# b cast to bf16 before its transposes, transposed as 4-byte words of two k each, with four rows of b in each partition

## The chip, the cores and the metric

The kernel runs on one core of one Trainium2 chip. A time is the device time of one execution in microseconds (us), the median of several runs; a span is that of the profiled execution, from its first to its last instruction, and is 1.6 to 2 us shorter. The kernel before takes 129.39 us (129.38 to 129.58, 3 runs). Engines are named as the profile names them: PE (TensorE matmuls), PEld (its weight loads), DVE (VectorE), ACT (ScalarE), POOL (GpSimd), SP (SyncE, which only issues DMAs here). On one core a run is told to be slow when it is over 1.5% above the fastest of its kernel.

## The reference

```python
batch, m, k, n = 16, 512, 512, 512
a: (batch, k, m) float32        b: (batch, n, k) float32
out = np.matmul(a.transpose(0, 2, 1), b.transpose(0, 2, 1)).astype(np.float32)
```

So out[m, n] is the sum over k of a[k, m] b[n, k]. The kernel's matmuls contract over partitions, so its tiles of both have k there. a has k first and is loaded as it is; b has n first, and the kernel transposes it on the chip. Per batch 1 MiB of a and 1 MiB of b come in, and 1 MiB goes out.

## The kernel before

Four k lie in each partition of a (`k = 4 ki + ko`). Rows of b lie 128 apart in a partition (`n = 128 no + ni`), so that a partition reads four separate runs of 2 KB. PE transposes b in f32, 16 times 128x128 per batch. DVE takes the transposes out of PSUM and casts them to bf16. ACT casts a. ACT and DVE take turns with the output.

```python
b_v = b.rearrange("b (no ni) k -> b ni no k", ni=P)
# a_pool 3, b_pool 3, ac_pool 4, bt_pool 3, o_pool 8, psum_t 4, psum_o 4 buffers; LAG = 6
for i in range(B):
    # ... b_sb and a_sb are loaded by DMA from SP; ACT casts a_sb to a_bf, four times 128x512
    b_sr = b_sb.rearrange("p no (pk rk) -> p no rk pk", rk=KO)
    for rk in range(KO):
        bt_ps = psum_t.tile([P, N], f32)
        for no in range(NO):
            nc.tensor.transpose(bt_ps[:, no * P:(no + 1) * P], b_sr[:, no, rk, :], identity)
        nc.vector.tensor_copy(bt_sb[:, rk, :], bt_ps)           # DVE, L73
    for rm in range(MO):
        for rk in range(KO):
            nc.tensor.matmul(o_ps, a_br[:, rk, rm, :], bt_sb[:, rk, :], ...)   # PE, L80
        # rm even: ACT copies o_ps to o_sb; rm odd: DVE does (L90)
    if i >= LAG:
        emit_out_dma(i - LAG)
```

Of the kernel before, what the change touches and what calls it, by code (L numbers as in the profile page):

```python
# [1 line left out]

# [5 lines left out]


@with_exitstack
def kernel(
    ctx: ExitStack,
    tc: tile.TileContext,
    a: bass.AP,
    b: bass.AP,
    out: bass.AP,
):
    nc = tc.nc
    P = 128  # L20
    B, K, M = a.shape
    _, N, _ = b.shape
    KO = K // P
    MO = M // P
    NO = N // P

    f32 = mybir.dt.float32
    cdt = mybir.dt.bfloat16

    a_v = a.rearrange("b (ki ko) m -> b ki ko m", ko=KO)  # L30
    b_v = b.rearrange("b (no ni) k -> b ni no k", ni=P)
    out_v = out.rearrange("b (mi mo) n -> b mi mo n", mo=MO)

    const = ctx.enter_context(tc.tile_pool(name="const", bufs=1))
    identity = const.tile([P, P], f32)
    make_identity(nc, identity)

    a_pool = ctx.enter_context(tc.tile_pool(name="a_pool", bufs=3))
    b_pool = ctx.enter_context(tc.tile_pool(name="b_pool", bufs=3))
    ac_pool = ctx.enter_context(tc.tile_pool(name="ac_pool", bufs=4))  # L40
    bt_pool = ctx.enter_context(tc.tile_pool(name="bt_pool", bufs=3))
    o_pool = ctx.enter_context(tc.tile_pool(name="o_pool", bufs=8))
    psum_t = ctx.enter_context(tc.tile_pool(name="psum_t", bufs=4, space=bass.MemoryType.PSUM))
    psum_o = ctx.enter_context(tc.tile_pool(name="psum_o", bufs=4, space=bass.MemoryType.PSUM))

    LAG = 6
    o_tiles = {}

    def emit_out_dma(j):
        nc.sync.dma_start(out_v[j], o_tiles.pop(j))  # L50

    for i in range(B):
        b_sb = b_pool.tile([P, NO, K], f32)
        nc.sync.dma_start(b_sb, b_v[i])
        a_sb = a_pool.tile([P, KO, M], f32)
        nc.sync.dma_start(a_sb, a_v[i])  # L56

        a_bf = ac_pool.tile([P, KO, M], cdt)
        for rk in range(KO):
            nc.scalar.copy(a_bf[:, rk, :], a_sb[:, rk, :])  # L60
        a_br = a_bf.rearrange("p rk (pm rm) -> p rk rm pm", rm=MO)

        b_sr = b_sb.rearrange("p no (pk rk) -> p no rk pk", rk=KO)
        bt_sb = bt_pool.tile([P, KO, N], cdt)
        for rk in range(KO):
            bt_ps = psum_t.tile([P, N], f32)
            for no in range(NO):
                nc.tensor.transpose(  # L68
                    bt_ps[:, no * P:(no + 1) * P],
                    b_sr[:, no, rk, :],  # L70
                    identity,
                )
            nc.vector.tensor_copy(bt_sb[:, rk, :], bt_ps)  # L73

        o_sb = o_pool.tile([P, MO, N], f32)
        o_tiles[i] = o_sb
        for rm in range(MO):
            o_ps = psum_o.tile([P, N], f32)
            for rk in range(KO):
                nc.tensor.matmul(  # L80
                    o_ps,
                    a_br[:, rk, rm, :],
                    bt_sb[:, rk, :],
                    start=(rk == 0),
                    stop=(rk == KO - 1),
                )
            if rm % 2 == 0:
                nc.scalar.copy(o_sb[:, rm, :], o_ps)  # L88
            else:
                nc.vector.tensor_copy(o_sb[:, rm, :], o_ps)  # L90

        if i >= LAG:
            emit_out_dma(i - LAG)

    for j in range(B - LAG, B):
        emit_out_dma(j)


# [1 line left out]
_INS = ['a', 'b']  # L100
_OUTS = [((16, 512, 512), 'float32')]


# [23 lines left out]
```

## Time and profile before

| | before |
|---|---|
| time, median | 129.39 us |
| span | 127.8 us |
| DMA: bytes, mean rate | 50.42 MB, 394 GB/s |
| busy share PE, DVE, ACT | 72%, 48%, 43% |
| packets of 2 KB | 8192, median 84 ns each |
| packets of 8 KB | 4105, median 309 ns each |

The packet figures are from the DMA packet records of the trace. The page's busy lines (tenths in 40 slices of the span) and its queue line show a DMA queue that is hardly ever idle:

```profile
PE   0099999999999995768767796877779777670000
DMA  3999999999999999999999999999999999999980
q1 hardware_dynamic: 13056, 50.33, 97.5%
```

The costliest groups of the same page, with busy us and mean ns of one:

```profile
L80 PE MATMUL o_ps<-bt_sb,a_bf 128*128 128x512 bf16 x248 | 59.0, 385 | 9.1 <-ACT a_bf L60 8.7
L73 DVE CAST bt_sb<-bt_ps 128x512 bf16<-128x512 f32 x64 | 40.0, 683 | 14.7 <-PE bt_ps L68 14.7
L68 PE MATMUL bt_ps<-identity,b_sb 128*128 128x128 f32 x256 | 35.7, 295 | 12.8 <-DMA b_sb<-in_b_dram 12.8
```

The list of waits (us in total, times, longest) says who sets the pace: ACT waits for a, and the transposes wait for b, that is for DMA.

```profile
ACT a_bf L60 <- DMA a_sb<-in_a_dram: 39.5, 13, 6.8
PE bt_ps L68 <- DMA b_sb<-in_b_dram: 12.8, 9, 6.4
```

In the first third data is there early, and the chain of waits (start us, us, what) shows what a batch takes when PE alone limits: 1.92 us of transposes and 3.45 us of matmuls, with nothing between them.

```profile
35.80 1.92 PE bt_ps L68 x16
37.72 0.22 PE o_ps L80
37.94 0.05 issue
37.99 3.18 PE o_ps L80 x14
41.18 1.92 PE bt_ps L68 x16
```

That is 5.4 us against some 7.5 us per batch of DMA.

### The profile page before, as it was taken

The page shows a single profiled execution, that of the slowest core. Times are in us where ns is not written, and L with a number is a line of the kernel's source. Part 1 is how long each engine was busy: PE and PEld are TensorE (multiplying, and loading weights), DVE is VectorE, ACT ScalarE, POOL GpSimd, SP SyncE. Part 2 cuts the span into 40 slices and gives each one's busy share as a digit, 9 for nine tenths or more (in the row PEclk, how much of TensorE's full clock was granted, in tenths as well). Part 3 has the DMA queues.
Part 4 walks back from the last instruction along what each step waited for, and adds up shares of the span by engine and source line. Part 5 has one row for each costly group of instructions (what it writes and reads, how often), then busy time and mean ns, then how long its engine had stood idle before and what let it go on. Part 6 is the DMA issues. An engine that isn't in the chain of part 4 may idle for free.

```text
span 127.8 us, 1405 instructions
## 1 busy us (share of the span) xinstructions
PE 92.5 (72%) x504; PEld 60.6 (47%) x512; DVE 61.5 (48%) x96; ACT 54.8 (43%) x97; POOL 0.7 (1%) x6
## 2 busy tenths in 40 slices
PE   0099999999999995768767796877779777670000
PEld 0094858678586763364634536353364634430000
DVE  0053668586774865463544727355472635640000
ACT  4026747646674635407163460816337072540000
POOL 2000000000000000000000000000000000000000
PEclk9999999999999999999999999999999999998555
DMA  3999999999999999999999999999999999999980
GB/s 90 402 370 422 406 399 420 382 409 398 404 417 415 417 419 394 416 410 429 420 410 423 406 436 405 416 426 413 427 402 431 412 424 418 426 428 428 426 346 36
DMA packets 13063, 50.42 MB, mean 394 GB/s; under 512 B 768, under 2 KB 768, under 8 KB 8960
## 3 DMA queue, kind: packets, MB, share of 16 engines
q1 hardware_dynamic: 13056, 50.33, 97.5%
q8 instruction: 4, 0.07, 0.2%
q14 instruction: 3, 0.02, 0.0%
HBM read 33.55 MB, written 16.78 MB: 394 GB/s over the span
## 4 chain that ended last, share of the span: by engine, by line
DMA 50%; PE 34%; SPq 3%; ACT 1%; issue 1%; DVE 1%; ACTq 0%
DMA a_sb<-in_a_dram 32%; PE o_ps L80 22%; DMA out_dram<-o_sb 13%; PE bt_ps L68 12%; DMA b_sb<-in_b_dram 4%; SPq L56 3%; ACT a_bf L60 1%; DVE o_sb L90 1%; ACT o_sb L88 0%; ACTq L60 0%; SPq L50 0%
## 5 line engine op out<-in xcount | busy, mean ns | idle before, releaser
L80 PE MATMUL o_ps<-bt_sb,a_bf 128*128 128x512 bf16 x248 | 59.0, 385 | 9.1 <-ACT a_bf L60 8.7
L60 ACT CAST a_bf<-a_sb 128x512 bf16<-128x512 f32 x64 | 34.9, 615 | 39.6 <-DMA a_sb<-in_a_dram 39.5
L73 DVE CAST bt_sb<-bt_ps 128x512 bf16<-128x512 f32 x64 | 40.0, 683 | 14.7 <-PE bt_ps L68 14.7
L68 PE MATMUL bt_ps<-identity,b_sb 128*128 128x128 f32 x256 | 35.7, 295 | 12.8 <-DMA b_sb<-in_b_dram 12.8
L80 PEld LDWEIGHTS <-a_bf 128*128 128x128 bf16 x256 | 27.3, 115 | 35.8 <-ACT a_bf L60 17.7
L68 PEld LDWEIGHTS bt_ps<-identity,b_sb 128*128 128x128 f32 x256 | 33.9, 211 | 17.5 <-PE o_ps L80 8.5
L90 DVE COPY o_sb<-o_ps 128x512 f32<-128x512 f32 x32 | 22.1, 692 | 38.9 <-PE o_ps L80 21.9
L88 ACT COPY o_sb<-o_ps 128x512 f32<-128x512 f32 x32 | 18.8, 586 | 19.0 <-PE o_ps L80 18.9
L60 ACT ACT_TABLE_LOAD x1 | 1.3, 1283 | 0.7 <-PEq L111 0.7
masks.py:199 POOL TENSOR_SCALAR_AFFINE_SELECT identity<-identity 128x128 f32<-128x128 f32 x1 | 0.3, 292 | 0.1
masks.py:197 POOL MEMSET identity<- 128x128 f32 x1 | 0.2, 204 | 0.3 <-POOLq L111 0.3
L111 POOL MEMSET const-bfloat16-1.0<- 128x1 bf16 x1 | 0.1, 101 | 0.0
L111 POOL MEMSET const-uint8-127<- 128x1 uint8 x1 | 0.1, 101 | 0.0
L111 POOL MEMSET const-float32-0.0<- 128x1 f32 x1 | 0.1, 98 | 0.2 <-issue 0.2
L111 POOL MEMSET const-float32-1.0<- 128x1 f32 x1 | 0.1, 98 | 0.0
## 6 DMA issues: line engine op xcount, KB each, us to landing
b_sb<-in_b_dram SPq DMA_DIRECT2D x16, 1024.0 KB, 15.4
a_sb<-in_a_dram SPq DMA_DIRECT2D x16, 1024.0 KB, 17.3
out_dram<-o_sb SPq DMA_DIRECT2D x16, 1024.0 KB, 17.4
```

The source lines that it names most:

```text
L56: nc.sync.dma_start(a_sb, a_v[i])
L60: nc.scalar.copy(a_bf[:, rk, :], a_sb[:, rk, :])
L68: nc.tensor.transpose(bt_ps[:, no * P:(no + 1) * P], b_sr[:, no, rk, :], identity,)
L73: nc.vector.tensor_copy(bt_sb[:, rk, :], bt_ps)
L80: nc.tensor.matmul(o_ps, a_br[:, rk, rm, :], bt_sb[:, rk, :], start=(rk == 0), stop=(rk == KO - 1),)
L88: nc.scalar.copy(o_sb[:, rm, :], o_ps)
L90: nc.vector.tensor_copy(o_sb[:, rm, :], o_ps)
L111: nc = _bacc.Bacc("TRN2", target_bir_lowering=False, num_devices=1)
```

## The change

The intent is to halve the transposes. DVE first casts b to bf16. Two neighbouring bf16 values are then read as one 4-byte word, and a transpose of such words moves two k at once: 8 transposes per batch and 2 evictions, not 16 and 4. The matmuls read each half of the words at a 4-byte step. Besides, b's rows now lie four to a partition (`n = 4 ni + no`), so that a partition reads one run of 8 KB. That leaves the transposed columns in another order, and the eviction puts them right by writing at a 16-byte step. Buffer counts and the lag of the stores change too.

```diff
-    b_v = b.rearrange("b (no ni) k -> b ni no k", ni=P)
+    b_v = b.rearrange("b (ni no) k -> b ni no k", no=NO)
-    # a_pool 3, b_pool 3, ac_pool 4, o_pool 8, LAG 6          (cut: five lines)
+    # a_pool 5, b_pool 5, ac_pool 3, bc_pool 2, o_pool 6, LAG 3
-        b_sr = b_sb.rearrange("p no (pk rk) -> p no rk pk", rk=KO)
-        bt_sb = bt_pool.tile([P, KO, N], cdt)
-        for rk in range(KO):
-            bt_ps = psum_t.tile([P, N], f32)
+        bc = bc_pool.tile([P, NO, K], cdt)
+        nc.vector.tensor_copy(bc, b_sb)
+        bc_w = bc.bitcast(f32).rearrange("p no (pk j) -> p no j pk", j=KO // 2)
+        bt_sb = bt_pool.tile([P, KO // 2, N], f32)
+        bt_w = bt_sb.rearrange("p j (ni no) -> p j no ni", no=NO)
+        for j in range(KO // 2):
+            bt_ps = psum_t.tile([P, NO, P], f32)
             for no in range(NO):
-                nc.tensor.transpose(bt_ps[:, no * P:(no + 1) * P], b_sr[:, no, rk, :], identity)
-            nc.vector.tensor_copy(bt_sb[:, rk, :], bt_ps)
+                nc.tensor.transpose(bt_ps[:, no, :], bc_w[:, no, j, :], identity)
+            nc.vector.tensor_copy(bt_w[:, j, :, :], bt_ps)
+        bt_h = bt_sb.bitcast(cdt).rearrange("p j (n h) -> p j h n", h=2)
...
-                    bt_sb[:, rk, :],
+                    bt_h[:, rk // 2, rk % 2, :],
```

## The prediction

> **What bounds the kernel now.** DMA. The page's DMA line is at 9 tenths in every slice but the first and last, the one data queue took 97.5% of the time of its 16 engines, and 50.33 MB moved at 394 GB/s over the 127.8 us span. PE (72%), DVE (48%) and ACT (43%) have slack: from 60 us on the timeline's period is 7.5 us per batch, set by "ACT a_bf waits for DMA a_sb" (39.5 us in all, the largest wait), in which PE works about 5.9 us. The chain passes through PE for 34%, but before 44 us, where DMA is full too.

> **On the bound.** No byte less moves. But b's rows are taken four to a partition, which reads one run of 8 KB, not four of 2 KB: 8192 packets of 2 KB become 2048 of 8 KB, like those of a and of the output. The trace's packet records have medians of 84 ns for 2 KB (mean 86.2) and 309 ns for 8 KB (mean 312.7). These fit 9 ns fixed + 37.5 ns per KB, and a 4-byte semaphore packet indeed takes 9 ns. [...] Saving per MiB of b: 4 x 84 - 309 = 27 ns per 8 KB by medians (32 by means), x 2048 / 16 engines = 3.5 to 4.1 us. All of that is on the limit.

> **Off the bound.** Transposes: 256 become 128, 120 ns each when dense (1.92 us for 16 in the chain): about 1 us of PE per batch saved. PSUM evictions by DVE: 64 become 32, now f32 written at a 16-byte step (0.68 us each if the step costs nothing). Added: a DVE cast 128x2048 f32 to bf16 in SBUF[...], per batch. DVE stays near 4 to 5 us per batch, under the 7.3 us of DMA. The output matmuls now read their moving operand at a 4-byte step; I expect 215 ns each as now. None of this is on the bound, so halving the transposes earns almost nothing.

> Buffers: only 8 DMAs are in flight (each issue waits for the landing of the eighth before it), so five input buffers can't be used fully. With LAG 3, stores 12 to 14 (about 7.4 us) cover the last batch's compute, which took 5.2 us from landing to store issue; so no bubble.

> **Predicted time.** 129.4 - 3.5 to 4.1 = 125.3 to 125.9 (pure stores ran at 428 GB/s, so a little more is possible). I say 125.2 us, 80% range 122.8 to 127.4. Chances: faster by over 2% 0.80, within 2% 0.12, slower 0.08.

> **What would show it right.** 6144 data packets of 8 KB at about 309 ns; none of 2 KB; mean GB/s 405 to 412; DMA still at 9 tenths throughout; PE's share near 60%; the wait "ACT a_bf for DMA a_sb" larger still; [...] L85 matmuls with unchanged mean.

> **What would make it wrong.** (1) The 4-byte step halves the matmul's rate: 16 x 0.43 + 1 = 8 us per batch, above DMA's 7.3; then PE bounds it, about 137 us. (2) Stores interleaved earlier with loads slow both, as in slices around 40 us, where 8 KB packets took 318 ns. (3) The last store waits for compute and leaves DMA idle. (4) More packets overlap, and it falls to 123.

The 9 ns are the trace's own. So are the 8 DMAs in flight: in the trace of before every issue came after the landing of the eighth before it, by 0.06 us at the closest (51.51 us, after 51.45). DVE's "4 to 5 us per batch" is a sum with the cast's term in it: the terms left, two evictions of transposes at 0.68 us and two output evictions at 0.69 us (the trace of before), make 2.7 us.

## More of the kernel before

The program text doesn't fix in which order an engine gets its instructions. The framework's scheduler settles that when the kernel is built, and the listing of the built kernel shows the outcome.

PE goes from one batch into the next by itself: while DVE still empties PSUM, the next transposes read b straight from the tile that DMA filled.

## The result

The changed kernel takes 141.05 us (median of 4 runs, 141.03 to 142.13) against 129.40 us for the kernel before in the same rounds: ratio 1.0925, interval 1.0888 to 1.0962. It is slower by some 9%; its output is correct. A ratio here and below is the recorded one of the two kernels' fast runs in the same rounds, and not quite the ratio of the medians quoted.

The page of after. Compare the DMA line: it is full as before for 32 slices, and then falls into holes. The second line is the TensorE clock that the throttle granted, in tenths.

```profile
PE   0099797884793947749385583957749395674940
PEclk9999999999689996899959999599999959999599
DMA  4999999999999999999999999999999980707016
q1 hardware_dynamic: 6912, 50.33, 87.0%
```

The packet records have 6154 packets of 8 KB with a median of 309 ns (and three longer records), and none of 2 KB. By the ends of these packets 90% of the bytes had moved at 110.4 us, against 112.8 us before: up to there DMA is ahead of the kernel before. The last 10% take 29 us. What is late is output.

```profile
L85 PE MATMUL o_ps<-bt_sb,a_bf 128*128 128x512 bf16 x249 | 70.8, 437 | 11.6 <-DVE bt_sb L77 10.3
L76 PE MATMUL bt_ps<-identity,bc 128*128 128x128 f32 x128 | 19.8, 300 | 31.6 <-DVE bc L67 31.6
L77 DVE COPY bt_sb<-bt_ps 128x512 f32<-128x512 f32 x32 | 31.7, 1066 | 12.6 <-PE bt_ps L76 12.6
L67 DVE CAST bc<-b_sb 128x2048 bf16<-128x2048 f32 x16 | 19.5, 1218 | 5.9 <-DMA b_sb<-in_b_dram 5.9
```

The transposes take half of what they took, 19.8 us and not 35.7 us. But each batch's first one now waits for the cast on DVE (31.6 us in all), and ACT and DVE hardly wait for DMA any more:

```profile
PE bt_ps L76 <- DVE bc L67: 31.6, 15, 6.9
ACT a_bf L60 <- DMA a_sb<-in_a_dram: 6.3, 2, 6.0
DVE bc L67 <- DMA b_sb<-in_b_dram: 5.9, 2, 5.5
```

The chain of waits between 58.98 and 75.93 us (two batches, from one cast to the next) shows a closed ring:

```profile
58.98 1.23 DVE bc L67
60.20 0.14 issue
60.34 0.73 PE bt_ps L76 x4
61.07 0.02 issue
61.09 1.08 DVE bt_sb L77
62.17 0.04 issue
62.21 3.81 PE o_ps L85 x16
66.02 0.02 issue
66.05 0.03 DVE o_sb L95
66.08 0.57 issue
66.66 1.23 DVE bc L67
...
69.89 3.34 PE o_ps L85 x8
73.23 0.23 issue
73.45 1.84 PE o_ps L85 x7
75.29 0.02 issue
75.32 0.04 DVE o_sb L95
75.35 0.57 issue
75.93 1.23 DVE bc L67
```

The cast of batch i+1 (1.23) is followed by its first four transposes (0.73), their eviction (1.08), the 16 matmuls (3.81) and DVE's last output eviction of that batch (0.69; the chain books 0.57 of it as "issue", and the next cast starts 0.08 before its recorded end). Only then comes the next cast. The listing of the built kernel shows why, and the trace has the same order: from batch 4 on, DVE's order is cast, two evictions of transposes, two output evictions, cast. The next b has landed long before (the cast waits for DMA only twice, at the start), but it stands in the queue behind an eviction that waits for PE, and PE's next transposes wait for the cast. In this trace each such cast starts within 0.1 us of the eviction's end, though its b had landed (as an example, batch 8's b at 59.97 us; its cast started at 66.66 us).

One turn of the ring takes 7.68 us, and 9.27 us where the clock was at half for 3.4 us, so that the matmuls took 5.4 us and not 3.8 (69.89 to 75.29). DMA's period would be some 7.4 us (an estimate: 3 MiB at the 425 GB/s of the middle slices).

### The profile page after: what moved, and what is told of

Same layout as the page of the kernel before. It is cut to its first block, busy times and chain, and to the rows that moved or that the text cites. A ratio compares the mean times of both kernels' runs of the same rounds, so it can differ in the third digit from the quotient of the medians.

```text
span 139.1 us, 1115 instructions
## 1 busy us (share of the span) xinstructions
PE 90.4 (65%) x377; PEld 46.7 (34%) x384; DVE 71.9 (52%) x80; ACT 53.4 (38%) x97; POOL 0.7 (1%) x6
## 3 DMA queue, kind: packets, MB, share of 16 engines
q1 hardware_dynamic: 6912, 50.33, 87.0%
## 4 chain that ended last, share of the span: by engine, by line
PE 55%; DVE 26%; issue 9%; DMA 5%; ACT 1%; SPq 0%
PE o_ps L85 48%; DVE bc L67 12%; DVE bt_sb L77 12%; PE bt_ps L76 7%; DMA a_sb<-in_a_dram 5%; DVE o_sb L95 1%; ACT a_bf L60 1%; SPq L54 0%
## 5 line engine op out<-in xcount | busy, mean ns | idle before, releaser
L85 PE MATMUL o_ps<-bt_sb,a_bf 128*128 128x512 bf16 x249 | 70.8, 437 | 11.6 <-DVE bt_sb L77 10.3
L85 PEld LDWEIGHTS <-a_bf 128*128 128x128 bf16 x256 | 30.9, 121 | 48.1 <-issue 27.5
L76 PE MATMUL bt_ps<-identity,bc 128*128 128x128 f32 x128 | 19.8, 300 | 31.6 <-DVE bc L67 31.6
L77 DVE COPY bt_sb<-bt_ps 128x512 f32<-128x512 f32 x32 | 31.7, 1066 | 12.6 <-PE bt_ps L76 12.6
L76 PEld LDWEIGHTS bt_ps<-identity,bc 128*128 128x128 f32 x128 | 17.2, 209 | 38.3 <-issue 36.6
L67 DVE CAST bc<-b_sb 128x2048 bf16<-128x2048 f32 x16 | 19.5, 1218 | 5.9 <-DMA b_sb<-in_b_dram 5.9
```

The source lines that it names most:

```text
L67: nc.vector.tensor_copy(bc, b_sb)
L76: nc.tensor.transpose(bt_ps[:, no, :], bc_w[:, no, j, :], identity)
L77: nc.vector.tensor_copy(bt_w[:, j, :, :], bt_ps)
L85: nc.tensor.matmul(o_ps, a_br[:, rk, rm, :], bt_h[:, rk // 2, rk % 2, :], start=(rk == 0), stop=(rk == KO - 1),)
```

## The experiments

Theory A: the loss is that ring; the place of the cast in DVE's order closes it, the lowered clock makes it longer. Rival B: the stepped reads and writes, with a clock that falls of itself. Rival C: the buffer counts and the earlier stores. Besides: is the DMA gain real? All kernels gave correct results.

| label | time, us | ratio to before |
|---|---|---|
| e1_cast_ahead | 126.75 | 0.980 |
| e2_warm | 135.93 | 1.050 |
| e3_old_pools | 134.11 | 1.034 |
| e4_rows_only | 134.22 | 1.038 |
| e5_two_casts | 165.13 | 1.277 |
| e6_words_only | 132.54 | 1.023 |
| e7_ahead_lag6 | 126.04 | 0.975 |
| e8_step_only | 129.59 | 1.002 |
| e9_rows_out_read | 126.43 | 0.978 |
| e10_rows_psum_step | 126.55 | 0.978 |
| e11_bc3 | 140.08 | 1.087 |
| e12_cast_pool | 127.11 | 0.982 |

The kernel before measured 129.24 to 129.57 us beside them. Each kernel ran 4 times (e7_ahead_lag6 5 times); one run of e3_old_pools and the profiled one of e12_cast_pool were slow. The medians in the table include these; the fast runs alone have 133.84 and 126.83 us.

### The cast one batch ahead

```diff
-        bc = bc_pool.tile([P, NO, K], cdt)
-        nc.vector.tensor_copy(bc, b_sb)
+        bc = bc_next                       # loaded and cast during the batch before
 ...
+        if i + 1 < B:
+            bc_next = cast_b(load_b(i + 1))
         o_sb = o_pool.tile([P, MO, N], f32)
-    bc_pool = ... bufs=2
+    bc_pool = ... bufs=3
```

> The changed kernel with one thing moved: the cast of batch i+1 is emitted before the output matmuls of batch i (bc in 3 buffers, not 2), so that on DVE it stands in front of at least the last PSUM eviction of batch i. Theory A (a serial loop through DVE: eviction of batch i, cast of i+1, transposes, eviction of the transposes, matmuls, and so on, 7.68 us warm and 9.27 us where the clock was lowered): the loop opens, DMA limits again, 122.5 to 126 us, the waits of PE for the cast near 0. Rival B (the matmuls' 4-byte step and the lowered clock by themselves): 138 us or more. Rival C (the new buffer counts and the stores 3 batches behind): 138 us or more.

126.75 us. The same work in another order on DVE is 14.3 us faster than the changed kernel, and 2.0% faster than before (ratio 0.9799, 0.9777 to 0.9821). The stepped reads and writes, the lag and all buffer counts but that of bc are the changed kernel's, so neither rival B nor rival C holds most of the loss. In its list of waits DMA is what ACT and DVE wait for again:

```profile
ACT a_bf L70 <- DMA a_sb<-in_a_dram: 30.4, 13, 6.1
DVE bc L59 <- DMA b_sb<-in_b_dram: 15.0, 7, 5.6
PE bt_ps L85 <- DVE bc L59: 10.3, 9, 7.0
```

The wait for the cast is not near 0, as I expected, but 10.3 us, of which the kernel's start has 7.0. The time misses the stated range by 0.75 us. The GB/s line of the page tells of a part of it: 428 417 197 218 in the last four slices, a hole at the end.

### That third buffer alone

```diff
-    bc_pool = ... bufs=2
+    bc_pool = ... bufs=3
```

> The run with the cast one batch ahead also gave bc a third buffer. Here only that: the changed kernel with bc in 3 buffers; the order listing of every engine's instructions is the same as in the changed kernel. Theory A (place of the cast in DVE's order): 141 us. Rival (two buffers of bc hold the cast back): 127 us or less.

140.08 us (139.76 to 141.84): the buffer is not what opened the ring.

### The cast on another engine

```diff
-        nc.vector.tensor_copy(bc, b_sb)
+        nc.gpsimd.tensor_copy(bc, b_sb)
```

> The same cast of b, in the same place of the program, on GpSimd, which has no other work in the loop: it can't stand behind an output eviction. DVE keeps its four evictions per batch in the order of the changed kernel. Theory A: the cast runs as soon as b has landed, the loop opens: 125.5 to 128 us (with the hole at the end that lag 3 leaves), if GpSimd takes under 5 us for one cast. If what matters is that there is a cast at all, or the stepped evictions and matmuls: 135 us or more.

127.11 us. One line, the slower engine (1.90 us for a cast, against 1.22 on DVE), and 14 us less. The group (only the kind of wait and the engine's own time are read from it):

```profile
L67 POOL CAST bc<-b_sb 128x2048 bf16<-128x2048 f32 x16 | 30.3, 1896 | 82.2 <-DMA b_sb<-in_b_dram 82.2
```

On POOL each of the 16 casts waits for b to land and for nothing else. The stepped eviction and the stepped matmuls are all still there, so rival B can't hold most of the loss.

### Two casts, a dose

```diff
         nc.vector.tensor_copy(bc, b_sb)
+        nc.vector.tensor_copy(bc, b_sb)
```

> A dose: the changed kernel with the cast of b done twice into the same tile (1.22 us more DVE work per batch; DVE would be busy some 92 us, far from full). Theory A (serial loop through the cast): every batch that is in the loop gets 1.2 us longer, and PE idles longer, so the lowered clock comes at least as often: 155 to 172 us, warm period 8.9 us. If the cast is not on the path: 141 us.

165.13 us: 24.1 us for 16 x 1.22 = 19.5 us of work on an engine that is busy 55% of the span. The rest goes with the clock: from batch 4 on every batch took 10.2 us, 8.9 us being the ring's length at the full clock (7.68 + 1.22), so each had a lowered clock in it, and the mean granted clock fell to 0.862 (0.924 in the changed kernel).

### The clock kept up

```diff
+    # (cut: the PSUM tile `warm`; psum_t has 3 buffers for it, not 4)
+        for _ in range(8):                 # result never read
+            nc.tensor.matmul(warm, a_br[:, 3, 3, :], bt_h[:, 1, 1, :], start=True, stop=True)
```

> The changed kernel with 8 extra 128x512 matmuls per batch into a PSUM bank that nobody reads, placed after the output matmuls, where PE waits some 2 us for the cast (psum_t has 3 banks, not 4, for it). They cost nothing if PE would idle there, and should keep the clock up. Theory A: the period is 7.68 us in every batch, no batch of 9.27 us, granted clock 0.99 or more, 129 to 132 us: the lowered clock is a part of the loss, some 9 to 11 us, and not its cause. Rival B with the clock as the only cause: 122 to 126 us. If the clock isn't kept up: 141 us or more.

135.93 us, so 5.1 us less than the changed kernel with 128 useless matmuls more. The clock stayed up, and the chain shows the ring bare, at 7.68 us in every turn from batch 5 on:

```profile
PEclk9999999999999999999999999999999999999999
60.51 1.23 DVE bc L70
68.19 1.23 DVE bc L70
```

It missed the range that I gave (129 to 132 us), because the useless matmuls were not free everywhere. The edit also moved DVE's order: the casts of batches 2 and 3 stand before both output evictions of the batch ahead of them (between the two in the changed kernel), so they were done early and the useless matmuls stood in PE's way. The matmuls of batch 3 end at 37.25 us, 5.1 us later than in the changed kernel (32.12 us). From there to the end of the last output matmul this run takes 91.7 us and the changed kernel 101.5 us. So the clock's share is more than the net 5.1 us: an estimate from these two traces is 9 to 10 us. The changed kernel's own trace agrees: its matmuls were lengthened by the lowered clock in six batches, by 1.4 to 1.6 us each, 9.4 us in all. That is the larger part of the 14.3 us that moving the cast won back. But it needs the ring: PE is idle for 2.0 us in each turn waiting for the cast, and in e1_cast_ahead, where the clock was lowered four times before the last matmul (mean granted clock 0.937), DMA still set the pace.

### Buffers and lag as before

```diff
-    a_pool 5, b_pool 5, ac_pool 3, o_pool 6; LAG = 3
+    a_pool 3, b_pool 3, ac_pool 4, o_pool 8; LAG = 6
```

> The changed kernel with the buffer counts and the store lag of the kernel before (a 3, b 3, cast a 4, out 8, lag 6). The order listing shows that this also moves the DVE order in the first seven batches: the cast stands between the two output evictions there, and after both from the eighth on. Theory A: the first half runs at the DMA's pace, the second half at 7.7 to 9.3 us per batch: 130 to 138 us. Rival C: all of the loss goes, 126 us or less. If buffers and order don't matter: 141 us.

134.11 us. The buffer counts do matter, but by way of the order. In the listing the casts of batches 2 to 6 stand between the two output evictions, those from batch 7 on after both. The casts start, in the trace, 6.09 us apart up to batch 6 (18.76, 24.85, 30.94, 37.03, 43.12), then 7.68 us (50.81), and 7.7 to 9.3 us from there on. The changed kernel turns at batch 4, where its listing does (25.07 to 32.76 us: 7.69). One step in the order of two instructions is 1.6 us per batch.

### The words without the new rows

```diff
-    b_v = b.rearrange("b (ni no) k -> b ni no k", no=NO)
+    b_v = b.rearrange("b (no ni) k -> b ni no k", ni=P)
-        bt_w = bt_sb.rearrange("p j (ni no) -> p j no ni", no=NO)
+        bt_w = bt_sb.rearrange("p j (no ni) -> p j no ni", no=NO)
```

> The other half of the change alone: the cast and the 4-byte words as changed, but b loaded as before (2 KB packets), so that the eviction of the transposes is contiguous (0.68 us, not 1.07). Theory A: the loop is 0.39 us shorter, 7.3 us warm and 8.9 us where the clock is lowered, and still bound by the loop: 134 to 138 us. If the stepped eviction is what broke it: 130 us or less. If it's the loop but the shorter loop falls under DMA's 7.5 us everywhere: 130 us.

132.54 us: outside both ranges, between them. The ring is there, with the eviction now 0.70 us and not 1.08, so 7.30 us:

```profile
56.91 1.23 DVE bc L67
59.03 0.70 DVE bt_sb L77
64.21 1.23 DVE bc L67
```

Turns at the full clock take 7.30 us and those with the lowered one 8.9 us, as expected. I had put too many of the latter: three of nine from batch 6 on, and the DMA queue (2 KB packets again) was busy 95.8%. The stepped eviction is a part of the ring's length, 0.38 us a turn, and not its cause.

### The new rows without the words, three ways

The DMA half alone needs some other way to put the columns right (the changed load of b, as in the diff above, is left out of the three cuts). First in the eviction of the f32 transposes, which writes bf16 at a step of 4 elements:

```diff
-            nc.vector.tensor_copy(bt_sb[:, rk, :], bt_ps)
+            nc.vector.tensor_copy(bt_sb[:, rk, :].rearrange("p (ni no) -> p no ni", no=NO),
+                                  bt_ps.rearrange("p (no ni) -> p no ni", no=NO))
```

> The kernel before with only b's load changed to four rows in each partition (8 KB packets), the f32 transposes as before, and the eviction of the transposes written at a 4-element step in bf16 to bring the columns into order. The DMA part of the prediction: 6144 packets of 8 KB, 3.5 to 4.1 us saved: 124.5 to 126.5 us. If the packet size gives nothing: 129 us. If the stepped bf16 eviction is dear (over 1.5 us each) a loop through DVE may show: over 129 us.

134.22 us: the second of the outcomes named. The eviction doubled:

```profile
L73 DVE CAST bt_sb<-bt_ps 128x512 bf16<-128x512 f32 x64 | 76.0, 1325 | 6.8 <-PE bt_ps L68 6.8
```

Four of them start 1.14 us apart, and with the two output evictions a turn through DVE and PE is again some 7.5 us (59.70 to 67.24 us). So this run did not isolate the DMA gain. The second way puts the columns right in the output evictions, which read PSUM at a 512-byte step:

```diff
+            o_pr = o_ps.rearrange("p (no ni) -> p ni no", no=NO)
-                nc.scalar.copy(o_sb[:, rm, :], o_ps)
+                nc.scalar.copy(o_w[:, rm, :, :], o_pr)     # DVE's the same; o_w: o_sb as p rm ni no
```

> The DMA half alone again, without a stepped write of the transposes (the run with it had evictions of 1.33 us and was bound by them): the kernel before with b's rows four to a partition; the transposes' eviction contiguous as before, and the order of the columns put right in the output evictions, which read PSUM at a 512-byte step and write SBUF contiguously. DMA theory: 8 KB packets save 3.5 to 4.1 us: 124.5 to 126 us, if the output evictions stay under 1.1 us each. Loop theory: if they cost 1.4 us or more on DVE or ACT, over 129 us.

126.43 us. The third lets PE write PSUM at a 16-byte step:

```diff
-                    bt_ps[:, no * P:(no + 1) * P],
+                    bt_ps.rearrange("p (ni no) -> p no ni", no=NO)[:, no, :],
```

> The same, with the order put right by PE: each transpose writes its 128 columns to PSUM at a 16-byte step, and all evictions are contiguous as in the kernel before. [...] If the transposes stay near 120 ns apart: 124.5 to 126 us. If they double to 240 ns: 1.9 us more of PE per batch, 5.4 + 1.9 = 7.3 us, near DMA's period, 125 to 130 us.

126.55 us. Both are missed by 0.4 to 0.6 us at the upper end, and both show the gain: 2.2% for one changed load and a free change of a pattern. Their groups are those of the kernel before (e10_rows_psum_step, then the second way):

```profile
L73 DVE CAST bt_sb<-bt_ps 128x512 bf16<-128x512 f32 x64 | 39.9, 682 | 12.4 <-PE bt_ps L68 12.3
L68 PE MATMUL bt_ps<-identity,b_sb 128*128 128x128 f32 x256 | 35.7, 295 | 10.6 <-DMA b_sb<-in_b_dram 10.5
```

```profile
L92 DVE COPY o_sb<-o_ps 128x512 f32<-128x512 f32 x32 | 22.1, 691 | 38.0 <-PE o_ps L81 21.1
L90 ACT COPY o_sb<-o_ps 128x512 f32<-128x512 f32 x32 | 18.8, 586 | 20.9 <-PE o_ps L81 20.8
```

### The 4-byte step of the matmuls alone

```diff
-        bt_sb = bt_pool.tile([P, KO, N], cdt)
+        bt_two = bt_pool.tile([P, KO // 2, N, 2], cdt)      # k pairs side by side
-                    bt_sb[:, rk, :],
+                    bt_sb[:, rk // 2, rk % 2, :],           # bt_sb: bt_two as p j n h -> p j h n
```

> The disputed cost by itself: the kernel before, with its transposed b laid out as in the change (two k side by side, so that the matmuls read their moving operand at a 4-byte step), loads and transposes as before. Matmuls start 226 to 228 ns apart where dense, not 215 (as in the changed kernel): 16 x 12 ns = 0.2 us per batch, hidden behind DMA. The eviction in bf16 at a 2-element step may cost DVE 0.7 to 1.35 us. If it stays under 1 us: 129 to 130 us. If it costs 1.3 us as at a 4-element step: 133 to 135 us.

129.59 us, ratio 1.002. Matmuls start 227 ns apart, not 216 (medians of both traces), and the eviction at a 4-byte step takes 731 ns, not 683. This was the risk that the prediction named first; it is 5% of a matmul and costs nothing here.

### The cast ahead, with stores six batches behind

```diff
-    a_pool 5, b_pool 5, o_pool 6; LAG = 3      (on top of the cast one batch ahead)
+    a_pool 4, b_pool 4, o_pool 8; LAG = 6
```

> The kernel with the cast one batch ahead (126.75 us), and stores 6 batches behind with 8 output buffers (4 and 4 input buffers to make room). In that run DMA ran at 417 to 430 GB/s until some 119 us and then at 200 GB/s, since only three stores lay ahead of the last batch's. Theory: with six there is no hole at the end, and the DMA part of the prediction comes out: 122.5 to 124.5 us. If the end isn't what costs: 126 to 127 us.

126.04 us, ratio 0.9747 (0.9720 to 0.9773): the fastest version, ahead of the kernel before by 2.5% and of the changed one by 15 us. The hole at the end is gone (the last five slices of its GB/s line are 425 423 428 417 61), but all that this run changed was worth 0.7 us, not 2 or more as I expected. 98% of the bytes had moved at 119.2 us, against 122.2 us before and 121.4 us in the run with lag 3. DMA limits it throughout: its queue took 97.1% of 16 engines' time.

## Why the prediction was wrong

- **What bounds the kernel before: right.** Versions whose compute stays out of the way and which still move b in 2 KB packets take what before takes (the run with the stepped matmuls alone, 129.59 us), and those with 8 KB packets take 126.0 to 126.8 us.
- **The DMA part: right, somewhat too large.** Packets became 8 KB at 309 ns, as said. I predicted 3.5 to 4.1 us; the three clean versions (126.04, 126.43, 126.55 us) are 3.5, 2.9 and 2.8 us below before in their own rounds.
- **The sizes of the single costs: right.** The cast took 1.22 us (1218 ns in the trace; the figure predicted for it was an estimate and is cut). DVE was busy 71.9 us / 16 = 4.5 us per batch ("4 to 5").
- **The step that failed: "DVE stays near 4 to 5 us per batch, under the 7.3 us of DMA ... None of this is on the bound".** I compared sums of busy time per engine, which bound a pipeline only if each engine can go on to the next batch by itself. Before, PE could: the transposes read what DMA had written. The change put DVE between DMA and PE, on the same queue on which the output evictions wait for PE (each cast from batch 4 on began within 0.1 us of the end of one). No engine was full (PE 65%, DVE 52%), yet the sum of one turn, 1.23 + 0.73 + 1.08 + 3.81 + 0.69 and the hand-overs, is 7.68 us at the full clock and 9.27 us at the lowered one, against DMA's 7.4. The prediction says nothing of the order in which DVE gets its instructions. Moving the cast in that order (e1_cast_ahead), taking it to another engine (e12_cast_pool) and doubling it (e5_two_casts) settle it.
- **Missed altogether: the clock.** PE idles 2.0 us per turn, and in the changed kernel the granted clock fell to a half for 3.41 us at a time. I had no term for it; it is worth some 9 to 10 us (an estimate from e2_warm and the changed kernel's trace), but only within the ring.
- **The named risks.** (1) was right in kind, a PE loop longer than DMA's period, and wrong in its cause: the step costs 11 ns per matmul (e8_step_only). (2) did not show: 8 KB packets kept a median of 309 ns. (3), which the text ruled out ("so no bubble"), is in part true even of the repaired kernel: with lag 3 the last slices fell to 197 and 218 GB/s. In that run the matmuls of batch 14 took 6.3 us from first to last, partly at the lowered clock, so batch 15 started late and its store was issued at 120.2 us. I had counted one batch's compute in isolation.
- **Left open.** Why the scheduler puts the casts of later batches behind both evictions was not looked into. No experiment varied how much PE work just holds the clock up; what the traces bracket stands in the list below.

## What to carry to other kernels

Busy shares tell whether an engine can be the limit, not whether a ring through several half-idle engines is. When a change puts an engine between a load and PE, follow one batch around: read the built order of that engine's queue, ask what each instruction stands behind, and add up the turn. If the sum is longer than the period of the real limit, emit the producer a batch ahead, or give it to an engine that waits for nobody; and let a gain on the real limit (here the 8 KB runs) go in by itself first.
